# Softmax heads of two attention mixers issued in pairs

## The chip, the cores and the metric

The kernel runs on one NeuronCore of one Trainium2 chip. The time is that of one execution on the device, in microseconds (us). Three runs of the kernel before gave 1333.37, 1333.61 and 1333.80 us, median 1333.61. The execution that was profiled took 1333.43 us, of which the trace covers a span of 1331.7 us.

Five engines work side by side, each through its own instruction queue in order: TensorE (PE; its weight loads are shown as PEld), VectorE (DVE), ScalarE (ACT), GpSimd (POOL) and SyncE (SP), which issues the transfers of the weights.

## The reference, cut to what matters

A decoder trunk of two layers on 256 tokens of width 1024. Each layer is a SwiGLU block, a mixer block with three token mixers side by side, a cross attention and a second SwiGLU block. The change touches two of the three mixers, which end in an ordinary softmax attention with heads of 64 features:

```python
# FoX, 6 heads: causal, with a decay c per head
logits = q @ k.T * 64**-0.5 + c[:, :, None] - c[:, None, :]
o_fox = softmax(where(causal, logits, -inf)) @ v
# DSA, 5 heads: only the 64 keys that an indexer picked for each query
o_dsa = softmax(where(picked & causal, q @ k.T * 64**-0.5, -inf)) @ v
# stick-breaking, 5 heads, is the third mixer and has no softmax
```

All arithmetic is float32. The dense projections are made of three TensorE passes each over a high and a low part of both factors (in the profile a pass is one matmul of line 139, 140 or 141); scores, transposes and value products of the mixers are plain float32.

## The kernel before

`mixer_cross(l)` writes one layer's mixers and cross attention. The 256 queries are two tiles of 128, and causality leaves 128 keys for the first and 256 for the second, so that one head's scores are one tile of 128 x 384 (`Q0`, `Q1`).

Heads go by two. A feature tile of 128 partitions holds two heads, 64 partitions each, and a head's score matmuls therefore read 64 partitions: partitions 0 to 63 for the first head of the two, 64 to 127 for the second. There are two per head, 128 and 256 columns wide (lines 664 and 668 for FoX, where line 664 adds the decay first; line 553 in `scores` for DSA; line 781 for stick-breaking). In this text the score matmuls of one head are a score run. FoX has three pairs of heads, DSA two pairs and a single head, stick-breaking the same.

Then, for each head by itself: DVE adds the mask from PSUM into an SBUF tile (lines 674 and 676, or 698), and `softmax_pv` (line 588) does the rest: maxima (594, DVE), exponentials with their sums (69, ACT), reciprocals (597) and scaling (599, DVE), three transposes of 128 x 128 (602, PE), one copy to SBUF (604, ACT), and `pv`: two value products into the PSUM tile that both heads share (611 and 612, PE). After both heads, `hsplit` splits the result for the output projection (154, DVE and ACT).

PE does not wait for these chains: dense projections that do not depend on them stand between the pieces, and their weights are prepared all the while, the high part by ACT (line 92), the low part by DVE or, for every third one, by POOL (line 86).

What sets the order. The source is traced in program order, and a planner then arranges each engine's queue when the program is built. It takes work in traced order where that is ready by its own estimate, and fills with later work where not. Three things tie its hands here: PSUM has two banks for scores (`qk`), two for transposes (`tr`) and one for value products (`ops`); there are five SBUF tiles `w384` for probabilities; and the helper `issue_after(x)` queues what its block issues on the engine of `x` behind `x`.

Of the kernel before, what the change touches and what calls it, by code (L numbers as in the profile page):

```python
# [9 lines left out]
F32 = mybir.dt.float32  # L10
F32R = mybir.dt.float32r
I32 = mybir.dt.int32
AF = mybir.ActivationFunctionType
OP = mybir.AluOpType
AX = mybir.AxisListType
# [17 lines left out]
def trunk(ctx: ExitStack, tc: tile.TileContext, x, mem, positions, ffn1_norm, ffn1_w_gu, ffn1_w_down,  # L33
# [3 lines left out]
    PE, ACT, DVE, POOL, SP = nc.tensor, nc.scalar, nc.vector, nc.gpsimd, nc.sync  # L37
# [10 lines left out]
    def qk_ps():  # L48
        return psum.tile([128, 512], F32, name="qk", bufs=2)

    def tr_ps():
        return psum.tile([128, 512], F32, name="tr", bufs=2)

    def o_ps():
        return psum.tile([128, 512], F32, name="ops", bufs=1)
# [11 lines left out]
    def tact(*a, **k):  # L67
        with tc.issue_after(tabs["load"].ins):
            i = ACT.activation(*a, **k)  # L69
        tabs["ops"].append(i)  # L70
# [89 lines left out]
    ident = consts.tile([128, 128], F32, name="ident")  # L160
# [55 lines left out]
    def scaled(k, src, h, lo, gi):  # L216

        g = gcol[:, gi * 8 + k:gi * 8 + k + 1]
        i = ACT.activation(h, src, AF.Copy, scale=g)
        DVE.scalar_tensor_tensor(lo, src, g, h.bitcast(F32), op0=OP.mult, op1=OP.subtract)  # L220
        return i
# [29 lines left out]
    with tc.tile_pool(name="start", bufs=1) as st:  # L251
# [10 lines left out]
        for k in (0, 1, 4, 5):  # L262
            ps = (tr_ps, qk_ps)[k // 4]()
            xps[k], xps[k + 2] = ps[:, :256], ps[:, 256:]
        ps = o_ps()
# [5 lines left out]
        for k in range(KD):  # L271
            last = scaled(k, xps[k], xh[k], xl[k], GI["ffn1"])
# [185 lines left out]
    Q0, Q1 = (0, 128), (128, 384)  # L458

    def mixer_cross(l):  # L460
# [4 lines left out]
        with tc.tile_pool(name="mix", bufs=1) as mp:  # L465
# [8 lines left out]
            def w384():  # L474
                return mp.tile([128, 384], F32, name="w384", bufs=5)
# [28 lines left out]
            def proj_feat(cls, bank=acc_ps):  # L504

                w = load_w([W[:, a:b] for a, b in cls])
                ps = bank()
                for s in range(sum(b - a for a, b in cls) // 128):
                    for k in range(KD):
                        mm3(ps[:, s * 256:(s + 1) * 256], cols(w[k], s), xg[k], k == 0, k == KD - 1)  # L510
                return ps
# [51 lines left out]
            for t in range(2):  # L563
                DVE.tensor_scalar(w8[:, t], pss[t][:, 256:264], rc[t], float(np.float32(8 ** -0.5)) * 0.125,
                                  op0=OP.mult, op1=OP.mult)
# [19 lines left out]
            POOL.tensor_tensor(dmask, dmask, cmask, op=OP.add)  # L585


            def softmax_pv(lg, v, h, ot):

                nm = mp.tile([128, 2], F32, name="nm", bufs=4)  # L590
                sm = mp.tile([128, 2], F32, name="sm", bufs=4)
                p = lg
                for t, (c0, c1) in enumerate((Q0, Q1)):
                    DVE.tensor_reduce(nm[:, t:t + 1], lg[:, c0:c1], axis=AX.X, op=OP.max, negate=True)
                    tact(p[:, c0:c1], lg[:, c0:c1], AF.Exp, bias=nm[:, t:t + 1], accum_out=sm[:, t:t + 1])
                rs = mp.tile([128, 2], F32, name="rsm", bufs=4)
                DVE.reciprocal(rs, sm)
                for t, (c0, c1) in enumerate((Q0, Q1)):
                    DVE.tensor_scalar(p[:, c0:c1], p[:, c0:c1], rs[:, t:t + 1], None, op0=OP.mult)
                ps = tr_ps()  # L600
                for j in range(3):
                    PE.transpose(ps[:, j * 128:(j + 1) * 128], p[:, j * 128:(j + 1) * 128], ident)  # L602
                pT = w384()
                ACT.activation(pT, ps[:, :384], AF.Copy)
                pv(ot, v, h, pT[:, 0:256], pT[:, 256:384])

            def pv(ot, v, h, p0, p1):

                o = ot[:, h % 2 * 256:(h % 2 + 1) * 256]
                c = slice(h // 2 * 128, h // 2 * 128 + 128)  # L610
                PE.matmul(o, v[0][:, c], p0, start=True, stop=False)  # L611
                PE.matmul(o[:, 128:256], v[1][:, c], p1, start=False, stop=True)  # L612

            def tok_v(pss, n):
                res = []
                for t in range(2):
                    v = mp.tile([128, 384], F32, name="vtok", bufs=4)
                    ACT.activation(v[:, :n], pss[t][:, :n], AF.Copy, scale=rc[t])
                    if n < 384:
                        POOL.memset(v[:, n:], 0.0)  # L620
                    res.append(v)
                return res
# [3 lines left out]
            for c in range(3):  # L626
                ps = proj_feat([(FOX0 + c * 256, FOX0 + (c + 1) * 256)])
# [6 lines left out]
            fv = tok_v(pss, 384)  # L634
# [12 lines left out]
            ps = tr_ps()  # L647
# [12 lines left out]
            for j in range(NFOX // 2):  # L660
                bank = [qk_ps() for _ in range(2)]
                for i, ps in enumerate(bank):
                    for c in (0, 256):
                        PE.matmul(ps[:, c:c + 256], sel[:, 2 * j + i], cneg, start=c == 0, stop=False)
                for c, n in ((0, 128), (256, 256)):
                    for i, ps in enumerate(bank):
                        b = slice(64 * i, 64 * i + 64)
                        PE.matmul(ps[:, c:c + n], fqk[j][b, c // 2:c // 2 + 128], fqk[3 + j][b, 0:n],  # L668
                                  start=False, stop=c == 256)
                ot = o_ps()  # L670
                for i, ps in enumerate(bank):
                    h = 2 * j + i
                    lg = w384()
                    DVE.scalar_tensor_tensor(lg[:, 0:128], ps[:, 0:128], cq[:, 0, h:h + 1], cmask[:, 0:128],
                                             op0=OP.add, op1=OP.add)
                    DVE.scalar_tensor_tensor(lg[:, 128:384], ps[:, 256:512], cq[:, 1, h:h + 1], cmask[:, 128:384],
                                             op0=OP.add, op1=OP.add)
                    softmax_pv(lg, fv, h, ot)
                ofox.append(hsplit(ot, 2))


# [8 lines left out]
            dv = tok_v(proj_tok(DSA0 + 640, 320), 320)  # L690
            odsa = []
            for j in range(3):
                nh = 2 if j < 2 else 1
                bank = scores(dT[0][j], dT[1][j], nh)
                ot = o_ps()
                for i, ps in enumerate(bank):
                    lg = w384()
                    DVE.tensor_tensor(lg, ps[:, :384], dmask, op=OP.add)
                    softmax_pv(lg, dv, 2 * j + i, ot)
                odsa.append(hsplit(ot, nh))  # L700

            gates = []
# [51 lines left out]
            for i, lst in enumerate((sq, sk)):  # L754
                ps = proj_feat([(SB0 + 320 * i, SB0 + 320 * i + 256)])
                for s in range(2):
                    o = t1()
                    DVE.scalar_tensor_tensor(o, ps[:, s * 256:(s + 1) * 256], (0.125, 1.0)[i], r[:, :256],
                                             op0=OP.mult, op1=OP.mult)
                    lst.append(o)  # L760
            ps = proj_feat([(SB0 + 256, SB0 + 320), (SB0 + 576, SB0 + 640)])
# [7 lines left out]
            for j in range(3):  # L769
# [31 lines left out]
                ot = o_ps()  # L801
# [8 lines left out]
            for k in range(0, KD, 2):  # L810
                mi = mp.tile([128, 2, 256], F32, name="mi", bufs=2)
                SP.dma_start(mi, mem[0, :, k * 128:(k + 2) * 128].rearrange("(t p) n -> p t n", p=128))
                ps = transposed([mi[:, t] for t in range(2)], 0)
# [24 lines left out]
            for c in range(4):  # L838
                w = load_w([w_out[l][:, c * 256:(c + 1) * 256]])
                for s in range(2):  # L840
                    ps = acc_ps()
# [24 lines left out]
            qT, pr, pT, vm, oc = [], [], [], [], []  # L866
# [37 lines left out]
            for c in range(4):  # L904
                w = load_w([ca_w_o[l][:, c * 256:(c + 1) * 256]])
                for s in range(2):
                    ps = acc_ps()
# [40 lines left out]
```

## Time and profile before

| | |
|---|---|
| median of three runs | 1333.61 us |
| the profiled execution | 1333.43 us, span 1331.7 us |
| PE busy | 1312.3 us, 99% of the span |
| weight loads (PEld) | 1276.6 us, 96% |
| DVE, ACT, POOL busy | 68%, 56%, 22% |
| granted TensorE clock | 0.9 or more of full speed in each of the 40 slices |
| chain that ended last | PE 88%, DVE 5%, ACT 2%, DMA 2% |

A row of the timeline is one instruction or a few equal ones that follow each other. A matmul's row lasts from its start to the end of its results, and the next one starts long before that: what a matmul costs PE is the distance from its start to the start of the next. Idle time in brackets counts only what lies behind the modelled end of the row before, so that a wait costs PE somewhat more than the bracket says. The order on PE, DVE, ACT and POOL changes between 259 and 412 us (layer 0) and between 910 and 1062 us (layer 1) and nowhere else; the stretches shown below reach a little further, 262 to 430 and 914 to 1080 us, to the end of the mixers' merge.

### The profile page before, as it was taken

Reading aid. Unit: us, or ns where it says so; the run is one execution under the profiler, and the core shown is the slowest. Engines: PE = TensorE matmul, PEld = TensorE weight load, DVE = VectorE, ACT = ScalarE, POOL = GpSimd, SP = SyncE. Lnnn points to the kernel's source line nnn. Section 1 sums busy time; section 2 is a strip of 40 time slices with the busy share of each in tenths; the row PEclk is TensorE's granted clock in tenths of the full one; section 3 lists DMA queues with packets and bytes.
Section 4 is the critical chain, followed back from the end, with each engine's and each line's share of the span. In section 5 each row is a group of like instructions: output and inputs, shape, how many; then the busy total and the mean of one; then the engine's idle time right before and its main releaser. Section 6 shows DMA issues by size and latency. Waiting matters only on the chain.

```text
span 1331.7 us, 26302 instructions
## 1 busy us (share of the span) xinstructions
PE 1312.3 (99%) x10746; PEld 1276.6 (96%) x10746; DVE 903.5 (68%) x1389; ACT 746.3 (56%) x1191; POOL 299.0 (22%) x267
## 2 busy tenths in 40 slices
PE   8999999999999999999999999999999999999997
PEld 7999998999899999999999999999989999999987
DVE  7866656975778876665666666569667787766644
ACT  6555544454766575554565554544557756655543
POOL 3211114421323222111121110334223230311100
PEclk9999999999999999999999999999999999999999
DMA  7665754544545555666655565646454565466551
GB/s 254 191 193 190 223 150 150 177 140 151 163 135 194 159 187 162 194 200 201 198 190 190 190 206 179 203 124 194 127 153 136 159 205 178 164 196 198 195 184 64
DMA packets 220712, 234.65 MB, mean 176 GB/s; under 512 B 8656, under 2 KB 209968, under 8 KB 220592
## 3 DMA queue, kind: packets, MB, share of 16 engines
q1 hardware_dynamic: 219904, 231.87, 54.7%
q8 instruction: 84, 1.38, 0.4%
q10 hardware_dynamic: 448, 0.57, 0.1%
q0 software_dynamic: 240, 0.55, 0.1%
q14 instruction: 36, 0.29, 0.1%
HBM read 231.91 MB, written 1.05 MB: 175 GB/s over the span
## 4 chain that ended last, share of the span: by engine, by line
PE 88%; DVE 5%; DMA 2%; ACT 2%; issue 2%; POOL 1%; SPq 0%; DVEq 0%; ACTq 0%; POOLq 0%
PE acc L139 27%; PE acc L140 27%; PE acc L141 27%; DVE wl L86 2%; PE qk L553 1%; PE ops L611 1%; ACT wh L92 1%; DMA wraw<-in_ffn_w_gu_dram 1%; DVE t L154 1%; PE qk L668 1%; DVE sc L583 0%; PE ops L612 0%; PE tr L602 0%; DMA wraw<-in_w_sb_out_dram 0%; POOL it L527 0%
## 5 line engine op out<-in xcount | busy, mean ns | idle before, releaser
L86 DVE TENSOR_TENSOR wl<-wraw,wh 128x1024 fp32r<-128x1024 f32 (+4 forms) x427 | 507.5, 1192 | 229.1 <-ACT wh L92 219.2
L92 ACT ACTIVATE wh<-wraw 128x1024 fp32r<-128x1024 f32 (+4 forms) x471 | 465.4, 994 | 262.2 <-PE acc L140 163.9
L141 PE MATMUL acc<-xh,wl 128*128 128x256 f32 x2032 | 563.8, 278 | 1.1 <-DVE wl L86 1.1
L140 PE MATMUL acc<-xl,wh 128*128 128x256 f32 x2032 | 564.0, 278 | 0.0
L139 PE MATMUL acc<-xh,wh 128*128 128x256 f32 x2032 | 563.0, 278 | 0.0
L141 PEld LDWEIGHTS acc<-xh,wl 128*128 128x128 f32 x2032 | 381.8, 188 | 3.3 <-DVE wl L86 1.5
L139 PEld LDWEIGHTS acc<-xh,wh 128*128 128x128 f32 x2032 | 381.3, 188 | 2.7 <-issue 2.7
L140 PEld LDWEIGHTS acc<-xl,wh 128*128 128x128 f32 x2032 | 382.2, 188 | 1.4 <-issue 1.0
L383 POOL TENSOR_TENSOR hm<-sg,gu 128x256 f32<-128x256 f32 x88 | 85.0, 967 | 385.3 <-ACT sg L69 385.3
L141 PE MATMUL acc<-hh,wl 128*128 128x256 f32 x528 | 145.3, 276 | 0.0
L140 PE MATMUL acc<-hl,wh 128*128 128x256 f32 x528 | 145.3, 276 | 0.0
L139 PE MATMUL acc<-hh,wh 128*128 128x256 f32 x528 | 144.3, 276 | 0.0
L86 POOL TENSOR_TENSOR wl<-wraw,wh 128x1024 fp32r<-128x1024 f32 (+4 forms) x44 | 90.6, 2059 | 228.9 <-ACT wh L92 208.5
L69 ACT ACTIVATE sg<-gu 128x256 f32<-128x256 f32 x88 | 36.7, 417 | 120.1 <-DVE gu L379 120.1
L141 PEld LDWEIGHTS acc<-hh,wl 128*128 128x128 f32 x528 | 99.1, 188 | 0.0
L140 PEld LDWEIGHTS acc<-hl,wh 128*128 128x128 f32 x528 | 99.1, 188 | 0.0
L139 PEld LDWEIGHTS acc<-hh,wh 128*128 128x128 f32 x528 | 98.4, 188 | 0.0
L379 DVE TENSOR_TENSOR gu<-acc,rs_r 128x512 f32<-128x512 f32 x88 | 60.3, 686 | 42.6 <-PE acc L141 42.4
L230 POOL TENSOR_TENSOR sqa<-sqa,sq 128x256 f32<-128x256 f32 x54 | 51.1, 945 | 148.7 <-ACT sq L225 147.3
L153 ACT ACTIVATE hh<-hm 128x256 fp32r<-128x256 f32 x88 | 36.1, 410 | 54.1 <-POOL hm L383 54.1
L154 DVE TENSOR_TENSOR hl<-hm,hh 128x256 fp32r<-128x256 f32 x88 | 37.0, 421 | 42.6 <-ACT hh L153 42.4
L141 PE MATMUL acc<-wh,xl 128*128 128x320 f32 (+1 forms) x192 | 61.4, 320 | 0.0
(283 smaller groups left out, 2002.6 us busy)
## 6 DMA issues: line engine op xcount, KB each, us to landing
wraw<-in_ffn_w_gu_dram SPq DMA_DIRECT2D x87, 1024.0 KB, 5.3
wraw<-in_w_in_dram SPq DMA_DIRECT2D x34, 1024.0 KB, 5.3
wraw<-in_ffn_w_down_dram SPq DMA_DIRECT2D x28, 896.0 KB, 4.8
wraw<-in_ffn_w_down_dram SPq DMA_DIRECT2D x18, 1024.0 KB, 5.2
wraw<-in_w_in_dram SPq DMA_DIRECT2D x20, 640.0 KB, 4.1
wraw<-in_ca_w_kv_dram SPq DMA_DIRECT2D x8, 1024.0 KB, 5.0
wraw<-in_w_out_dram SPq DMA_DIRECT2D x8, 1024.0 KB, 5.0
wraw<-in_ca_w_q_dram SPq DMA_DIRECT2D x4, 1024.0 KB, 5.2
```

Source lines behind the costliest of these rows:

```text
L69: i = ACT.activation(*a, **k)
L86: share["last"] = eng.tensor_tensor(lo, raw, h.bitcast(F32), op=OP.subtract)
L92: ACT.activation(h, raw, AF.Copy)
L139: PE.matmul(ps, a[0], b[0], start=first, stop=False)
L140: PE.matmul(ps, a[0], b[1], start=False, stop=False)
L141: PE.matmul(ps, a[1], b[0], start=False, stop=last)
L153: ACT.activation(h, src, AF.Copy)
L154: DVE.tensor_tensor(lo, src, h.bitcast(F32), op=OP.subtract)
L230: POOL.tensor_tensor(n, sqacc[0], sq, op=OP.add)
L379: DVE.tensor_tensor(gu, ps.rearrange("p (i n) -> p i n", i=2), rb2(r), op=OP.mult)
L383: POOL.tensor_tensor(hm, sg, gu[:, 1], op=OP.mult)
L553: PE.matmul(ps[:, c:c + n], q[b, qs], k[b, 0:n], start=True, stop=True)
```

## The change

`softmax_pv` takes the score tiles of both heads of a pair (or the one of the last DSA head) and runs in three passes: normalise all heads, then transpose all heads and copy each, then all value products. The two mixers collect their tiles in `lgs` and call it once for each pair. Two `issue_after` blocks are put around the transposes and the value products; they name an instruction of DVE and one of ACT, while the blocks hold PE instructions alone.

```diff
-            def softmax_pv(lg, v, h, ot):
+            def softmax_pv(lgs, v, h0, ot):
...
+                for p in lgs:
+                    nm = mp.tile([128, 2], F32, name="nm", bufs=4)
+                    sm = mp.tile([128, 2], F32, name="sm", bufs=4)
+                    for t, (c0, c1) in enumerate((Q0, Q1)):
+                        DVE.tensor_reduce(nm[:, t:t + 1], p[:, c0:c1], axis=AX.X, op=OP.max, negate=True)
+                        tact(p[:, c0:c1], p[:, c0:c1], AF.Exp, bias=nm[:, t:t + 1], accum_out=sm[:, t:t + 1])
+                    rs = mp.tile([128, 2], F32, name="rsm", bufs=4)
+                    DVE.reciprocal(rs, sm)
+                    for t, (c0, c1) in enumerate((Q0, Q1)):
+                        last = DVE.tensor_scalar(p[:, c0:c1], p[:, c0:c1], rs[:, t:t + 1], None, op0=OP.mult)
+                pTs = []
+                for p in lgs:
+                    ps = tr_ps()
+                    with tc.issue_after(last.ins):
+                        for j in range(3):
+                            PE.transpose(ps[:, j * 128:(j + 1) * 128], p[:, j * 128:(j + 1) * 128], ident)
+                    pT = w384()
+                    last_copy = ACT.activation(pT, ps[:, :384], AF.Copy)
+                    pTs.append(pT)
+                with tc.issue_after(last_copy.ins):
+                    for i, pT in enumerate(pTs):
+                        pv(ot, v, h0 + i, pT[:, 0:256], pT[:, 256:384])
...
+                lgs = []
                 for i, ps in enumerate(bank):
...
-                    softmax_pv(lg, fv, h, ot)
+                    lgs.append(lg)
+                softmax_pv(lgs, fv, 2 * j, ot)
```

No instruction is added or taken away. What moves is the order, and three places show it. Names carry buffer numbers: `qk_3606` and `qk_3607` are the score banks of the two heads of one pair.

PE, layer 0, the second DSA pair. Before, the first head's score run stands alone among the projections (`acc`), and the second head's comes after 50 more rows:

```order
L141 MATMUL acc_4073<-xh3_85,wl_4066 128x256
L139 MATMUL acc_4073<-xh4_86,wh_4069 128x256
L553 MATMUL qk_3606<-t1_3470,t1_3376 128x128
L553 MATMUL qk_3606<-t1_3470,t1_3376 128x256
L140 MATMUL acc_4073<-xl4_94,wh_4069 128x256
L141 MATMUL acc_4073<-xh4_86,wl_4070 128x256
```

Now:

```order
L140 MATMUL acc_3882<-xl3_93,wh_3874 128x256
L141 MATMUL acc_3882<-xh3_85,wl_3875 128x256
L553 MATMUL qk_3606<-t1_3470,t1_3376 128x128
L553 MATMUL qk_3606<-t1_3470,t1_3376 128x256
L553 MATMUL qk_3607<-t1_3470,t1_3376 128x128
L553 MATMUL qk_3607<-t1_3470,t1_3376 128x256
L139 MATMUL acc_3882<-xh4_86,wh_3878 128x256
```

Both heads' scores now follow each other, and an earlier projection (`acc_3882` in place of `acc_4073`) lies around them.

PE, layer 1, the first stick-breaking pair (`qk_12365`, `qk_12366`), which comes after DSA. Before, a DSA head's value products cut the first head's run in two, and the second head's run stands elsewhere:

```order
L139 MATMUL acc_12505<-osp_11404,wh_12481 128x256
L781 MATMUL qk_12365<-t1_12182,t1_12245 128x256
L611 MATMUL ops_11735<-w384_11752,vtok_11670 128x256
L612 MATMUL ops_11735<-w384_11752,vtok_11673 128x128
L781 MATMUL qk_12365<-t1_12182,t1_12245 128x128
L140 MATMUL acc_12505<-osp_11405,wh_12481 128x256
```

Now (line 781 has become 792):

```order
L141 MATMUL acc_12306<-wh_12301,xl7_97 128x320
L792 MATMUL qk_12365<-t1_12182,t1_12245 128x256
L792 MATMUL qk_12366<-t1_12182,t1_12245 128x256
L792 MATMUL qk_12365<-t1_12182,t1_12245 128x128
L792 MATMUL qk_12366<-t1_12182,t1_12245 128x128
L139 MATMUL acc_12485<-osp_11286,wh_12477 128x256
```

The value products are gone from between, since DSA is over by then, and the two heads stand together.

PE, layer 0, the transposes of the last, single DSA head (`w384_3663`; `osp` is the split output of a mixer, `mi` the memory tokens). Before:

```order
L611 MATMUL ops_3612<-w384_3649,vtok_3547 128x256
L612 MATMUL ops_3612<-w384_3649,vtok_3550 128x128
L602 MATMUL tr_3675<-ident_73,w384_3663 128x128
L243 MATMUL tr_4454<-ident_73,mi_4452 128x128 x4
L602 MATMUL tr_3675<-ident_73,w384_3663 128x128 x2
L139 MATMUL acc_4432<-osp_3163,wh_4404 128x256
```

Now (line 602 has become 606):

```order
L141 MATMUL acc_4010<-xh5_87,wl_4007 128x256
L606 MATMUL tr_3675<-ident_73,w384_3663 128x128
L139 MATMUL acc_4010<-xh6_88,wh_4006 128x256
L606 MATMUL tr_3675<-ident_73,w384_3663 128x128 x2
L140 MATMUL acc_4010<-xl6_96,wh_4006 128x256
L141 MATMUL acc_4010<-xh6_88,wl_4007 128x256
```

They have moved from the merge of the FoX output (`acc_4432`) to an earlier projection (`acc_4010`), with projection matmuls before, between and behind them.

## Rows read from the trace of the kernel before

**Rows 1.** The page, busy time by engine.
```profile
PE 1312.3 (99%) x10746; PEld 1276.6 (96%) x10746; DVE 903.5 (68%) x1389; ACT 746.3 (56%) x1191; POOL 299.0 (22%) x267
```

**Rows 2.** Busy us by stretch; last three columns: granted clock, DMA share, GB/s.
```profile
262.00:430.00 168.00, 165.22 (x1330) 158.47 (x1330) 123.09 (x194) 105.64 (x190) 47.52 (x31) 1.00 0.51 156
914.00:1080.00 166.00, 163.81 (x1316) 156.94 (x1315) 124.56 (x202) 107.45 (x189) 53.75 (x32) 1.00 0.51 156
469.00:479.00 10.00, 10.00 (x61) 8.90 (x60) 5.66 (x13) 7.75 (x17) 0.00 (x0) 1.00 0.65 213
```

**Rows 3.** Timeline of PE, waits: start, duration, row, [idle before <-releaser].
```profile
343.13 0.33 PE L602 MATMUL tr<-ident,w 128*128 128x128 f32 x1 [0.39 <-DVE w L599]
344.50 0.39 PE L139 MATMUL acc<-osp,wh 128*128 128x256 f32 x1 [0.38 <-DVE t L726]
...
425.69 0.39 PE L140 MATMUL acc<-t,wh 128*128 128x256 f32 x1 [0.66 <-DVE t L154]
...
996.47 0.33 PE L602 MATMUL tr<-ident,w 128*128 128x128 f32 x1 [0.20 <-DVE w L599]
996.64 0.60 PE L243 MATMUL tr<-ident,mi 128*128 128x128 f32 x4
997.07 0.38 PE L602 MATMUL tr<-ident,w 128*128 128x128 f32 x2
998.22 0.39 PE L139 MATMUL acc<-osp,wh 128*128 128x256 f32 x1 [0.77 <-DVE t L726]
...
1078.06 0.38 PE L140 MATMUL acc<-t,wh 128*128 128x256 f32 x1 [1.05 <-DVE t L154]
```

**Rows 4.** Timeline of PE: both heads' score runs together; then two heads' value products.
```profile
365.11 0.28 PE L139 MATMUL acc<-xh,wh 128*128 128x256 f32 x1
365.32 0.93 PE L781 MATMUL qk<-t,t 64*128 64x256 f32 x8
...
366.40 0.28 PE L141 MATMUL acc<-xh,wl 128*128 128x256 f32 x1
...
366.65 0.28 PE L140 MATMUL acc<-xl,wh 128*128 128x256 f32 x1
366.77 0.59 PE L611 MATMUL ops<-az,vtok 128*128 128x256 f32 x2
...
368.19 0.28 PE L139 MATMUL acc<-xh,wh 128*128 128x256 f32 x1
```

**Rows 5.** Timeline of PE, layer 0: one head's score run between projections.
```profile
312.78 0.28 PE L141 MATMUL acc<-xh,wl 128*128 128x256 f32 x1
...
313.23 0.28 PE L139 MATMUL acc<-xh,wh 128*128 128x256 f32 x1
313.44 0.92 PE L553 MATMUL qk<-t,t 64*128 64x128 f32 x4
...
314.51 0.28 PE L141 MATMUL acc<-xh,wl 128*128 128x256 f32 x1
```

**Rows 6.** Timeline of PE, layer 1: a score run cut by value products.
```profile
989.52 0.28 PE L139 MATMUL acc<-osp,wh 128*128 128x256 f32 x1
...
991.84 0.28 PE L141 MATMUL acc<-osp,wl 128*128 128x256 f32 x1
```

**Rows 7.** Timeline of DVE, layer 0: one DSA head, mask add and scaling.
```profile
310.95 0.56 DVE L698 TENSOR_TENSOR w<-qk,dmask 128x384 f32<-128x384 f32 x1
...
313.95 0.55 DVE L599 TENSOR_SCALAR w<-w,rsm 128x128 f32<-128x128 f32 x2
```

**Rows 8.** Timelines of POOL and DVE, layer 0: a low part beside a scaling.
```profile
284.62 2.38 POOL L86 TENSOR_TENSOR wl<-wraw,wh 128x1024 fp32r<-128x1024 f32 x1 [7.69 <-DVE rsm L597]
284.64 2.71 DVE L599 TENSOR_SCALAR w<-w,rsm 128x128 f32<-128x128 f32 x2
```

**Rows 9.** Timeline of PE, layer 0, cross attention: a run of transposes.
```profile
469.62 1.03 PE L890 MATMUL tr<-ident,t 128*128 128x128 f32 x8
470.49 1.04 PE L890 MATMUL qk<-ident,t 128*128 128x128 f32 x8
```

More of the change, by code (lines that the diff above doesn't have):

```diff
@@ L585, in mixer_cross @@
             POOL.tensor_tensor(dmask, dmask, cmask, op=OP.add)
-            def softmax_pv(lg, v, h, ot):
[L590 to L605, printed above, removed]
+            def softmax_pv(lgs, v, h0, ot):
[21 more added lines that the diff above has]
+                        pv(ot, v, h0 + i, pT[:, 0:256], pT[:, 256:384])
@@ L695, in mixer_cross @@
                 ot = o_ps()
+                lgs = []
                 for i, ps in enumerate(bank):
@@ L698, in mixer_cross @@
                     DVE.tensor_tensor(lg, ps[:, :384], dmask, op=OP.add)
-                    softmax_pv(lg, dv, 2 * j + i, ot)
+                    lgs.append(lg)
+                softmax_pv(lgs, dv, 2 * j, ot)
                 odsa.append(hsplit(ot, nh))
```

## The prediction

> **What bounds the kernel now.** The page's list of engines comes first: PE is busy for 1312.3 us, 99% of the span [rows 1], and no other engine comes near. So PE's own queue sets the time, and an edit can act in two ways only: on how long PE's instructions take, and on the gaps in which PE waits. [...] Then PE's timeline, which shows where these gaps are. There are nine. Four belong to one place in each layer, the transposes of the last DSA head and the matmul behind them (0.39, 0.38, 0.20 and 0.77 us, sum 1.74); two to the end of the merge, where PE waits for the last split (0.66 and 1.05) [rows 3]; the other three share what is left, 4.97 - 1.74 - 1.71 = 1.52 us. A gap costs more than its bracket: the second of the two transposes at 997.07 starts 0.11 later, and from there to 998.22 are 1.04 us where 0.11 is usual, so that a bracket of 0.77 cost 0.93. I add 0.16 to each.
>
> No more than about 5 + 9 x 0.16 = 6.4 us is therefore to be had from waits. The rest must come from PE's work, and the number of instructions is unchanged. So the question is whether any of them costs less in its new neighbourhood.
>
> **What moves and what it costs.** *Transposes and value products.* Four transposes in a run take from 996.64 to 997.07, 0.11 us each [rows 3]. In the group that is there now, one, then four, then two, none costs more for being in a group of one or two. Two heads' value products take 368.19 - 366.65 less two matmuls, 1.54 - 0.23 = 1.31 us [rows 4]; by half, 0.66 each. To issue six transposes or four products together, which is what the change says, I put at nothing: PE does the same work in the same time.
>
> *Score runs.* These change price. PE's step is (313.23 - 312.78) / 4 = 0.1125 us. One head's score run alone takes PE from 313.23 to 314.51, less two steps: 1.28 - 0.225 = 1.055 us [rows 5]. Both heads' runs next to each other take 366.40 - 365.11, less two steps: 1.29 - 0.225 = 1.065 us [rows 4]. The second head is free when it follows at once: the two read different halves of the partitions, and PE works on both. It is free in the order first head, first head, second head, second head too, since that is how the four stand there. Pairing the softmax makes the planner ask for both score banks at once, and the order shows four pairs joined that were apart: the second DSA pair and the first stick-breaking pair, in both layers. Each saves 2 x 1.055 - 1.065 = 1.045 us, together 4.18.
>
> In layer 1 the stick-breaking run was cut in two besides: from 989.52 to 991.84, less two steps and a head's products, 2.32 - 0.225 - 0.66 = 1.44 us [rows 6], 0.38 over a whole run. That goes as well. In the third FoX pair of layer 0 the new order issues the first head's narrow matmul, then two decay matmuls, then the other three: the pair is joined, but cut. It saves between nothing and 1.045 us; I take 1.045 - 0.38 = 0.66, the price of the cut just seen. The other pairs stay as they were. Sum of PE's work: 4.18 + 0.38 + 0.66 = 5.2 us less.
>
> *Waits that go.* At the four places of the last DSA head nothing stood between its value products and its transposes that PE could do meanwhile. In the new order projection matmuls lie before, between and behind these transposes, and the merge that waited with them comes later than DSA. I count all four as gone: 1.74 + 4 x 0.16 = 2.4 us. If the cover failed, they would come back, no more. The waits at the end of the merge are a chain behind the last eviction, whose order is untouched; they stay.
>
> *Waits that come.* The change adds none by name, but PE must find both heads normalised where it found one. Queued behind a transpose that waits is all of PE. One head's chain on DVE, from mask add to the end of the scaling, takes 314.50 - 310.95 = 3.55 us with exponentials on ACT in between [rows 7]. Two heads in the same queues take at least one more scaling, 4.1 us, and at most twice the time, 7.1. Against this stands the PE work that the new order puts between the last score and the first transposes. It is shortest for the first DSA pair of layer 0: 34 steps and a joined score run, 34 x 0.1125 + 1.065 = 4.9 us. There the wait is between 0 and 2.2 us, and I take 1. For the first DSA pair of layer 1 it is 6.4 us by the same count, and for the other ten groups 9 to 15, above the upper bound.
>
> What can still hold a chain up is a neighbour on DVE. At 284.64 the two scalings of a head took 2.71 us in place of the 0.55 of [rows 7], while POOL's subtraction ran from 284.62 to 287.00 [rows 8]: 2.16 us more. They ended at 287.35, so that at least one of them could finish only when POOL was done. [...]
>
> POOL is busy for 47.52 of 168 us and 53.75 of 166 [rows 2], some 30%. Of the twelve groups of both layers 3 to 4 would be hit, at half the price of 2.16 us on average, 4 us in all, but the groups have 2 us and more in hand. I take 1 us for it, and 0 to 8 for both kinds of wait together.
>
> **The sum.** 1333.43 (the profiled execution, 0.18 below the median of the runs) - 5.2 - 2.4 + 2.0 = 1327.8 us, 0.4% less.
>
> **The rivals.**
>
> *All of it, without new waits.* For it: the long distances above. 1333.4 - 5.2 - 2.4 = 1325.8, and with the cut FoX run fully joined and the three small waits gone, 1333.4 - 5.6 - 2.4 - 2.0 = 1323.4.
>
> *Given back at the merge.* PE reaches the merges earlier by 2.5 us and more in each layer, and both waits there are released by DVE [rows 3]. If DVE's queue sets that moment, and not the chain, the score gain returns as wait: 1333.4 - 2.4 + 1 = 1332.0, no change. For it: DVE is the busiest engine behind PE, 123.09 of 168 us [rows 2]. Against it: that is 73%, and the softmax and stick-breaking work of DVE moves forward with its chains.
>
> *The joined runs do not pay.* The second head's matmuls can wait in the run for their bank or operands, and the price of [rows 4] is from stick-breaking alone. Then 1333.4 - 2.4 + 2.0 = 1333.0, no change. Against it: the order of both kernels has such runs of line 553 too.
>
> *Slower: both heads behind one lock.* With the scalings of two heads side by side, one blocked scaling delays six transposes. The place is the scaling of each of the twelve groups, the price 2.16 us. The gain of 5.2 + 2.4 - 1 = 6.6 us is eaten by three hits in full, and it decides for slower by 0.2% from 9.3 us on, between four and five hits. Six would give 1333.4 - 6.6 + 13.0 = 1339.8. For it: [rows 8] show such a hit just ahead of a head's transposes. Against it: the hits must fall where there is no lead.
>
> [...]
>
> **How the numbers follow.** Forecast 1325 to 1331: 0.58. Better than that: 0.10. Given back: 0.12. Joined runs that do not pay: 0.06. Slower by the lock: 0.13. By the clock: 0.01. A difference under 0.2%, 2.7 us, can't be told from none here. So faster 0.68, same 0.18, slower 0.14. The range reaches from 1323.5, the best case, to 1335, past the two cases without gain and up to the first hits of the lock that outweigh it; it leaves out 0.04 below and 0.14 above. Of the forecast alone it would be 1325 to 1331.
>
> **What would show it.** Right: the four joined score runs at 1.06 us each; no wait at the last DSA head's transposes; PE's idle time in the two stretches at or below 5 us; all transposes and products at their old price. Wrong: gaps of 1 us and more before transposes with DVE's scaling as releaser and POOL's subtraction beside it (the lock); longer gaps at the end of the merge (given back); second heads in joined runs that cost 0.3 us or more (the price); a clock below 1.00.

## The result and the profile after

The changed kernel takes 1322.96 us (median of four runs, 1322.72 to 1323.02). The ratio to the kernel before is 0.992, with a 95% interval of 0.9908 to 0.9931: 10.7 us less than 1333.70, the median of four runs. The forecast was 1327.8 us with a range from 1323.5, so the direction was right, the size was half of what came, and the time lies just below the range. The profiled execution took 1323.02 us, 10.41 less than that of before. All times here are medians; one execution of e10_late_4, which took 5323.44 us, is left out.

The same views as before, of the kernel after. First the page's list of engines, then the table by stretch over the same work (it begins and ends some us earlier now):

```profile
PE 1305.2 (99%) x10746; PEld 1273.2 (96%) x10746; DVE 894.0 (68%) x1389; ACT 746.3 (56%) x1191; POOL 295.8 (22%) x267
```

```profile
262.00:424.30 162.30, 161.71 (x1331) 156.72 (x1330) 116.04 (x191) 106.64 (x191) 48.38 (x31) 1.00 0.53 162
908.40:1069.60 161.20, 160.37 (x1315) 155.23 (x1314) 121.60 (x202) 106.01 (x187) 51.13 (x33) 1.00 0.52 162
```

The two stretches are 5.7 and 4.8 us shorter than in [rows 2], and nothing outside them changed by more than 0.1. PE's idle time in them fell from 4.97 us (2.78 in layer 0 and 2.19 in layer 1, span less PE busy in [rows 2]) to 0.59 + 0.83 = 1.42 us. DVE is busy for 9.5 us less over the span with the same instructions. Three waits are left, from PE's timeline:

```profile
420.05 0.38 PE L140 MATMUL acc<-t,wh 128*128 128x256 f32 x1 [0.59 <-DVE t L154]
921.38 0.47 PE L671 MATMUL qk<-cneg,sel 128*128 128x256 f32 x2 [0.27 <-DVE w L684]
1067.65 0.39 PE L140 MATMUL acc<-t,wh 128*128 128x256 f32 x1 [0.56 <-DVE t L154]
```

Two are the ends of the merges, one is new (the decay of a FoX pair, at 921.38, which waits for a score bank that DVE's mask add frees). The four at the last DSA head [rows 3] are gone, as forecast. But the three small ones are gone too, and the end of layer 1's merge waits half as long. A joined score run, the second DSA pair of layer 0, PE's timeline:

```profile
299.08 0.28 PE L141 MATMUL acc<-xh,wl 128*128 128x256 f32 x1
299.29 0.93 PE L553 MATMUL qk<-t,t 64*128 64x128 f32 x8
300.15 0.39 PE L139 MATMUL acc<-xh,wh 128*128 128x256 f32 x1
300.37 0.28 PE L140 MATMUL acc<-xl,wh 128*128 128x256 f32 x1
...
301.63 0.49 PE L606 MATMUL tr<-ident,w 128*128 128x128 f32 x3
...
302.20 0.27 PE L606 MATMUL tr<-ident,w 128*128 128x128 f32 x1
...
302.43 0.38 PE L606 MATMUL tr<-ident,w 128*128 128x128 f32 x2
```

From 299.08 to 300.37, less two steps, are 1.29 - 0.225 = 1.065 us for both heads, the price of [rows 4]. Below it are the six transposes of the pair before: three, then one, then two, with projections between. "Issued together" in the source is not together on PE.

The two table loads that bracket the sigmoids show a larger move, which the prediction had not looked at. They are ACT's line 64, behind the last exponential of DSA and of stick-breaking. Timeline of ACT, layer 0, before:

```profile
341.80 1.28 ACT L64 ACT_TABLE_LOAD   x1
...
398.90 1.28 ACT L64 ACT_TABLE_LOAD   x1
```

and after:

```profile
314.36 1.28 ACT L64 ACT_TABLE_LOAD   x1
...
383.83 1.28 ACT L64 ACT_TABLE_LOAD   x1
```

DSA ends 27.4 us earlier and stick-breaking 15.1, while PE's projections moved by 5.7 at most. Before, PE waited right behind these points: at 344.50 [rows 3] and in this row, both released by DVE's gate product (line 726), which reads the sigmoids.

```profile
403.23 0.36 PE L139 MATMUL acc<-osp,wh 128*128 128x256 f32 x1 [0.51 <-DVE t L726]
```

### The profile page after: what moved, and what is told of

Same layout as the page of the kernel before. It is cut to its first block, busy times and chain, and to the rows that moved or that the text cites. A ratio compares the mean times of both kernels' runs of the same rounds, so it can differ in the third digit from the quotient of the medians.

```text
span 1321.3 us, 26329 instructions
## 1 busy us (share of the span) xinstructions
PE 1305.2 (99%) x10746; PEld 1273.2 (96%) x10746; DVE 894.0 (68%) x1389; ACT 746.3 (56%) x1191; POOL 295.8 (22%) x267
## 4 chain that ended last, share of the span: by engine, by line
PE 94%; DVE 2%; DMA 1%; issue 1%; POOL 1%; ACT 1%; DVEq 0%; ACTq 0%; POOLq 0%
PE acc L139 29%; PE acc L141 28%; PE acc L140 28%; DVE wl L86 1%; PE qk L553 1%; PE ops L618 1%; PE qk L675 1%; DMA wraw<-in_ffn_w_gu_dram 1%; DVE t L154 1%; PE ops L619 1%; PE tr L606 0%; POOL it L527 0%; DMA wraw<-in_w_in_dram 0%; PE qk L861 0%; PE qk L792 0%
## 5 line engine op out<-in xcount | busy, mean ns | idle before, releaser
L86 DVE TENSOR_TENSOR wl<-wraw,wh 128x1024 fp32r<-128x1024 f32 (+4 forms) x427 | 512.7, 1204 | 224.2 <-ACT wh L92 210.9
```

The costliest lines, as they stand in the source:

```text
L86: share["last"] = eng.tensor_tensor(lo, raw, h.bitcast(F32), op=OP.subtract)
```

## The experiments

Two theories of the waits. Theory A, a lead: when heads go one by one, the mixers' chains end too late for the projections that stand behind them; in the new order they end earlier. Rival B, meetings: the waits came from operations of DVE that met a subtraction on POOL, as in [rows 8], and the new order happens to have fewer. B had support at once. This view of one tile's instructions gives count and min/median/max in ns of the scaling, before and after:

```profile
L599 DVE TENSOR_SCALAR w<-w,rsm x44: 281/344/2447, 262.2 to 996.3; 128x128 f32<-128x128 f32 x22, 128x256 f32<-128x256 f32 x22
```

```profile
L600 DVE TENSOR_SCALAR w<-w,rsm x44: 261/314/350, 264.9 to 965.5; 128x128 f32<-128x128 f32 x22, 128x256 f32<-128x256 f32 x22
```

Before, 8 of the 44 took over 0.5 us; after, none did. That holds for the scalings alone: the DVE operations of stick-breaking meet POOL in both kernels.

**What of the edit makes the order.** One edit on the kernel before, in both mixers:

```diff
                 for i, ps in enumerate(bank):
                     lg = w384()
                     DVE.tensor_tensor(lg, ps[:, :384], dmask, op=OP.add)
-                    softmax_pv(lg, dv, 2 * j + i, ot)
+                    lgs.append(lg)
+                for i, lg in enumerate(lgs):
+                    softmax_pv(lg, dv, 2 * j + i, ot)
```

> The kernel before with one edit: the mask adds of both heads of a pair are written ahead of the first head's softmax; maxima, exponentials, transposes, copy and value products stay head by head. Theory A (the gain comes from the order in which the planner sets PE's queue once the second head's mask add no longer stands behind the first head's copy, and not from grouped transposes or grouped value products): the order on all five engines is that of the changed kernel, so 1323.0 us, within 0.5. Rival B (grouping six transposes and four products is worth something in itself): between 1326 and 1333.7 us.

Measured: 1323.60 us, ratio 0.9921 (0.9906 to 0.9936), the whole of the gain. Instruction for instruction the order on the five engines is that of the changed kernel; only buffer numbers differ. The planner gives the same order when the second head's mask add is written behind the first head's transposes, and the old one when it is written behind the first head's copy. Without the two `issue_after` blocks the order of the changed kernel stays as it is. (None of these three versions was timed.) So neither grouped transposes nor grouped value products nor the blocks gave anything: the second head's mask add (one DVE instruction in DSA, two in FoX), written ahead of one copy, did it all.

**What a joined run saves.** In the changed kernel, three times:

```diff
-                        b = slice(64 * i, 64 * i + 64)
+                        b = slice(0, 64)
```

> The changed kernel with one number changed: the second head of every pair reads its scores from partitions 0 to 63, those of the first head (so the second head's scores are not its own). Order and instruction counts are unchanged. Theory A (two adjacent heads cost 1.06 us because PE works on both halves of the partitions at once): the 16 fully joined pairs of both layers rise from 1.06 us towards 2.11, each by 0.7 to 1.05 us, 11 to 17 us in all: 1334 to 1340 us. Rival B (a lone head costs 1.055 us because of a fixed price at the two ends of a score run, paid once per run): the joined runs stay near 1.06 us and the time stays at 1323 us.

Measured: 1334.32 us, ratio 1.000 (0.999 to 1.001), 10.7 us above e1_mask_first, which ran beside it. The run of the rows above now, PE's timeline:

```profile
302.73 0.28 PE L141 MATMUL acc<-xh,wl 128*128 128x256 f32 x1
302.94 1.57 PE L553 MATMUL qk<-t,t 64*128 64x128 f32 x8
304.44 0.39 PE L139 MATMUL acc<-xh,wh 128*128 128x256 f32 x1
304.67 0.28 PE L140 MATMUL acc<-xl,wh 128*128 128x256 f32 x1
```

1.94 - 0.225 = 1.71 us. So both were partly right: of the 1.045 us that a joined pair saves, 0.65 come from the two halves of the partitions and 0.40 from a run that begins and ends once instead of twice. 16 pairs x 0.65 and 0.43 for the cut one make 10.8, as measured (10.7); PE's waits are the same in both, 1.4 us.

**Pairs in one mixer alone.** FoX keeps the pairs, DSA hands over single heads, and the other way round:

```diff
-                    lgs.append(lg)
-                softmax_pv(lgs, dv, 2 * j, ot)
+                    softmax_pv([lg], dv, 2 * j + i, ot)
```

> The changed kernel with the pairs in FoX alone; DSA hands its heads to the softmax one by one, mask add and all, as before. Score runs against the kernel before: the first stick-breaking pair joined in both layers (2 x 1.045), its cut in layer 1 gone (0.38), the third FoX pair of layer 0 joined but cut (0.43), a new cut in the second DSA pair of layer 0 (-0.38): 2.5 us less. Theory A (waits go because the mixers' chains end earlier against PE's projections): with half of the pairs the last stick-breaking head still comes earlier, most of the waits at the merges and at the last DSA head go, 3 to 4.5 us: 1326.5 to 1328.5 us. Rival B (waits go because scalings no longer meet POOL's subtractions on DVE): the waits stay wherever a DSA scaling still takes over 0.4 us; 1330 us or more.

> The changed kernel with the pairs in DSA alone; FoX hands its heads to the softmax one by one as before. Score runs against the kernel before: the second DSA pair joined in both layers, the first stick-breaking pair joined in layer 0 (3 x 1.045) and joined but cut in layer 1 (about 0.7), a new cut of the lone DSA head and of a FoX run in layer 0 and (-0.4 to -0.8): 3.1 us less. Theory A (earlier chains): the waits at the last DSA head and two of those at the merges go, 3 to 4 us: 1326.5 to 1328 us. Rival B (fewer meetings of scaling and POOL): FoX scalings still meet POOL as before, 5 of the 8 long scalings stay, and the waits with them: 1330 us.

Measured: 1326.65 us (0.9943, 0.9928 to 0.9958) and 1325.13 us (0.9932, 0.9917 to 0.9947): 7.5 and 9.0 us less, the first as A gave, the second 1.4 us below it, which was not traced. The two don't add up (16.5 against 10.6), since either alone takes away nearly all waits: 1.4 us of brackets are left in both stretches together, as with both. With DSA alone 7 scalings still meet POOL. Timeline of e4_dsa_pairs, layer 1, POOL, then DVE, then PE:

```profile
971.71 2.49 POOL L86 TENSOR_TENSOR wl<-wraw,wh 128x1024 fp32r<-128x1024 f32 x1 [9.73 <-ACT wh L92]
```

```profile
972.69 1.85 DVE L600 TENSOR_SCALAR w<-w,rsm 128x128 f32<-128x128 f32 x2
```

```profile
976.17 0.27 PE L606 MATMUL tr<-ident,w 128*128 128x128 f32 x1
976.43 0.38 PE L606 MATMUL tr<-ident,w 128*128 128x128 f32 x2
```

The scaling lost 1.3 us, and the transposes that need it have no bracket: a meeting without a wait. The changed kernel has one too, in the first stick-breaking pair of layer 1, where this DVE operation took 2.53 us in place of 0.95 beside POOL and the matmuls behind it have no bracket:

```profile
989.74 2.53 DVE L154 TENSOR_TENSOR spl<-az,sph 128x768 fp32r<-128x768 f32 x1
```

Both speak for A.

**Other draws.** The count that gives POOL every third low part, moved by one and by two places, in both kernels:

```diff
         share["pool"] = 3
+        share["n"] += 1
```

> The kernel before with another draw of the low parts: POOL takes every third as before, but counted from one place later, so that other subtractions meet the scalings on DVE. No other edit. Theory A (in the kernel before the mixers' chains end too late for PE, wherever POOL's subtractions fall): the waits at the last DSA head's transposes, behind the sigmoids and at the merges are there again, 4 to 7 us over both layers, and the time is 1332 to 1336 us. Rival B (the waits came from the few scalings and stick-breaking operations that met POOL): the waits move or go with the hits, and the time may fall to 1329 us.

> The same with the count moved by two places. Theory A: 1332 to 1336 us, waits at the same places. Rival B: as low as 1329 us, and other places than in the run moved by one.

> The changed kernel with the count of the low parts moved by one place. Score runs: the third FoX pair of layer 0 falls apart (+0.43), that of layer 1 is joined but cut (-0.43). Theory A (the paired order gives the chains a lead, whatever POOL meets): no waits over 0.5 us except at the end of the two merges, 1321.5 to 1325 us, 8.5 to 12 below the kernel before moved by one. Rival B (this order happened to miss POOL): scalings meet POOL again and 2 to 5 us of waits come back, 1325 to 1328 us.

> The changed kernel with the count moved by two places. Score runs: the third FoX pair joined in full in both layers (-0.6 and -1.03), the second DSA pair apart by three rows in both (+2.09). Theory A: no waits over 0.5 us except at the end of the merges, 1322 to 1325.5 us, 8 to 12 below the kernel before moved by two. Rival B: 1325.5 to 1329 us, with waits behind scalings that took over 0.5 us.

| draw | before, us | after, us | difference | waits before / after, us | scalings over 0.5 us |
|---|---|---|---|---|---|
| as it was | 1333.70 | 1322.96 | -10.7 | 5.0 / 1.4 | 8 / 0 |
| by one | 1335.24 | 1323.73 | -11.5 | 5.9 / 1.5 | 8 / 0 |
| by two | 1346.74 | 1329.89 | -16.9 | 8.8 / 2.8 | 10 / 0 |

(Waits are the brackets of both stretches. A draw also moves work outside them, so only differences within a row count. By two, both kernels missed the time that A gave; the difference is larger than A gave, and part of it is the clock: the kernel before has a mean granted clock of 0.991 to 0.996 in this draw, all others of the table 0.998 or 0.999.) The sign and the places hold in every draw: all three kernels of before wait for the last DSA head's scaling and behind the sigmoids, in both layers. The meetings differ as well, so this does not part A from B.

By two, the changed kernel also missed A's "no waits over 0.5 us": it waits for the second stick-breaking pair in both layers, 0.85 us each. e8_after_n2, layer 0, POOL, DVE and PE:

```profile
362.04 2.41 POOL L86 TENSOR_TENSOR wl<-wraw,wh 128x1024 fp32r<-128x1024 f32 x1
362.73 2.54 DVE L154 TENSOR_TENSOR spl<-az,sph 128x768 fp32r<-128x768 f32 x1 [0.36 <-ACT sph L153]
365.32 0.50 PE L805 MATMUL qk<-spl,negu 128*128 128x512 f32 x1 [0.85 <-DVE spl L154]
```

That is a wait as B has it, in the changed order: the operation lost 1.6 us, and here its reader had no such lead.

**No meetings at all.** In the kernel before:

```diff
-        share["pool"] = 3
+        share["pool"] = 0
```

> The kernel before with all low parts of the mixers on DVE: POOL has none, so that no scaling can meet one. DVE gets some 16 more subtractions of 1.2 us in each layer. Theory A (the chains of single heads end too late for PE by themselves): the waits of PE for the last DSA head's scaling and behind the sigmoids are still there, 1.5 us or more in each layer, though no scaling takes over 0.4 us: 1334 to 1345 us. Rival B (the waits were made by scalings that met POOL): these waits are gone, and what remains is for low parts (line 86): 1327 to 1334 us.

Measured: 1342.85 us, ratio 1.0069 (1.0054 to 1.0084). The time lies where A put it, but says little, since the granted clock fell to 0.50 in both layers of the profiled execution (340 to 346 and 1000 to 1010 us); in the kernel before it is 1.00 in both stretches [rows 2]. The scaling, and PE's waits in layer 0 (us in total, times, longest):

```profile
L599 DVE TENSOR_SCALAR w<-w,rsm x44: 268/314/351, 265.1 to 1007.0; 128x128 f32<-128x128 f32 x22, 128x256 f32<-128x256 f32 x22
```

```profile
PE tr L602 <- DVE w L599: 1.2, 1, 1.2
PE acc L140 <- DVE t L154: 0.7, 1, 0.7
PE ops L611 <- DVE w L698: 0.6, 1, 0.6
PE acc L139 <- DVE t L726: 0.5, 1, 0.5
```

No scaling takes over 0.351 us, and the waits for the scaling and behind the sigmoids are there, the first larger than in the kernel before (1.2 for 0.39); together 8.0 us of brackets. So PE waits there without any meeting. But DVE's list is longer here by the subtractions it took over, so that this run alone doesn't show what made the waits of the kernel before.

**Where the waits of the kernel before come from.** Its own trace goes further. First the last DSA head of layer 1, ACT and then DVE, ahead of PE's wait at 996.47 [rows 3]:

```profile
994.14 0.49 ACT L604 ACTIVATE w<-tr 128x384 f32<-128x384 f32 x1 [0.99 <-PE tr L602]
995.46 0.56 DVE L783 TENSOR_TENSOR zm<-qk,smask 128x384 f32<-128x384 f32 x1 [1.91 <-PE qk L781]
996.13 0.55 DVE L599 TENSOR_SCALAR w<-w,rsm 128x128 f32<-128x128 f32 x2
```

ACT copied the transposes of the head before, and only then, at 994.53, began the last head's exponentials; DVE stood idle for 1.91 us ahead of this head's scaling, which took its usual 0.55. PE, which released the copy and the mask add of 995.46, had no wait of its own between 925 and 996 us, so that no meeting has a part in this. In layer 0 DVE met POOL in a scaling at 335.59, but stood idle for 1.07 us behind it, before the last head's maxima at 340.48, so that this loss did not reach PE's wait at 343.13 either; and the sigmoids of 344.50 and 998.22 stand behind the same exponentials. Ahead of the wait at 403.23 POOL had done nothing for 16 us, and DVE had been waiting for PE at 395.91, so that no earlier loss was carried over:

```profile
403.16 1.30 POOL L728 TENSOR_TENSOR t<-t,t 128x512 f32<-128x512 f32 x1 [16.19 <-DVE t L726]
```

These five waits, 2.2 of the 5.0 us of brackets, are late chains, as A has it. The wait at 359.72, for the first stick-breaking pair of layer 0, is not. POOL, DVE, ACT and PE:

```profile
355.38 2.60 POOL L86 TENSOR_TENSOR wl<-wraw,wh 128x1024 fp32r<-128x1024 f32 x1 [3.44 <-ACT wh L92]
355.64 3.15 DVE L787 SCALAR_TENSOR_TENSOR az<-zm,az 128x768 f32<-128x768 f32 x1
358.82 0.84 ACT L153 ACTIVATE sph<-az 128x768 fp32r<-128x768 f32 x1 [3.05 <-DVE az L787]
359.72 0.50 PE L793 MATMUL qk<-sph,negu 128*128 128x512 f32 x1 [0.83 <-ACT sph L153]
```

The DVE operation lost 2.2 us (its like takes 0.95), ACT stood idle for 3.05 us until it was done, and PE lost 1.00 us: without the meeting the operand would have been there in time. Without meetings (e9_before_nopool) this wait is not in the list, and in the other draws the waits for a stick-breaking pair stand behind such a meeting too. So A holds for the waits at the last DSA head and behind the sigmoids, B for this one; what made the two waits at the ends of the merges and the small one for a low part was not traced.

**How long the lead is.** The changed kernel with transfers in the lone stick-breaking head, two and four rounds of:

```diff
+                    SP.dma_start(zf[:, 1], zf[:, 0])
+                    SP.dma_start(zf[:, 0], zf[:, 1])
                 tact(az, zm, AF.Exp)
```

> The changed kernel with a delay in the lone stick-breaking head of each layer: ahead of its last exponential its tile is copied four times to and fro by SP's transfers, which load no computing engine. [...] The sigmoids that the merge waits for stand behind this exponential on ACT: the table switch ahead of them is at 383.83 us in the changed kernel, and the merge wants them some 9 us later. Theory A (a lead of about 9 us): a delay below 9 us costs nothing, 1323 to 1324 us; what is over 9 us comes back as waits of PE at the merge. Rival B (a late chain does no harm, PE has other work): 1323 us.

> [...] Theory A: 3 to 11 us of waits at the merge in each layer, on the matmuls that read the split outputs and released by DVE's gate product: 1329 to 1345 us, and the wait is the delay less about 9 us. Rival B: 1323 to 1325 us.

Measured: 1329.35 us (0.9965, 0.9952 to 0.9979) and 1351.82 us (1.0133, 1.0118 to 1.0148). The 3 to 11 us of waits that A gave with eight copies rest on the author's estimate of one transfer, which no run had shown. In layer 0 a transfer took 3.3 us with four and 3.2 us with eight (median from issue to landing; 2.1 to 4.9 in both). The exponential on ACT and PE's waits behind it, layer 0, with four and with eight:

```profile
397.33 0.52 ACT L69 ACTIVATE az<-zm 128x384 f32<-128x384 f32 x1 [3.32 <-DMA zm<-zm]
```

```profile
397.90 0.70 PE L618 MATMUL ops<-az,vtok 128*128 128x256 f32 x2 [1.21 <-ACT az L69]
400.66 0.37 PE L139 MATMUL acc<-osp,wh 128*128 128x256 f32 x1 [1.24 <-DVE t L737]
```

```profile
410.01 0.52 ACT L69 ACTIVATE az<-zm 128x384 f32<-128x384 f32 x1 [14.17 <-DMA zm<-zm]
```

```profile
410.58 1.22 PE L618 MATMUL ops<-az,vtok 128*128 128x256 f32 x2 [13.26 <-ACT az L69]
```

Undelayed, this exponential starts at 383.29. 14.0 us later costs 1.2 us at the value products and brings back the wait behind the sigmoids (1.24); another 12.7 us cost another 12.1. Up to some 13 us of delay are free, and then, in layer 0, it is one for one: A, though the lead is longer than the 9 us expected. In layer 1 eight copies cost only 6.2 us at the value products, where the planner had put more merge work ahead of them. It knows of the transfers and had moved the value products back in both layers, so this is the lead that it could make use of, not that of an untouched order. A part of the times is the clock: with eight it was 0.50 from 411 to 416 us, behind the wait; with four its mean from 262 to 430 us was 0.99.

**All pairs joined.** Order edges on PE in the changed kernel; in `scores`, and alike in the other places:

```diff
-                    for i, ps in enumerate(bank):
+                    for i in reversed(range(nh)):
...
+                            if lead:
+                                es.enter_context(tc.issue_after(lead.ins))
+                            m = PE.matmul(bank[i][:, c:c + n], q[b, qs], k[b, 0:n], start=True, stop=True)
+                        lead = lead or m
```

> The changed kernel with every score pair joined by order edges on PE: in the indexer, DSA and stick-breaking the first head's matmuls are queued behind the second head's first one, in FoX both heads' score matmuls behind the second head's decay matmuls. Against the changed kernel that joins two indexer pairs of layer 0 (2 x 1.045), the second FoX pair of both layers and the third of layer 1 (3 x 1.03) and takes the cut out of the third of layer 0 (0.6): 5.8 us less, 1317.2 us, if no wait comes. Rival (a first head that must wait for the second bank holds up PE): each such wait costs up to the distance between the two heads' mask adds, 0.7 us, and the time stays at 1320 us or more.

Measured: 1319.13 us, ratio 0.9887 (0.9872 to 0.9901): faster than both kernels, 4 us below the changed one by the ratios. The second FoX pair of layer 0, and what came back, PE's timeline:

```profile
260.39 0.93 PE L681 MATMUL qk<-t,t 64*128 64x128 f32 x8
...
266.72 0.89 PE L611 MATMUL tr<-ident,w 128*128 128x128 f32 x5 [0.96 <-DVE w L605]
```

The runs are joined as expected (the sum of their prices is 5.8 us lower). The wait at 266.72 is not the rival's, which spoke of banks: four scalings from 263.21 took 3.91 us while POOL worked until 266.43. Here is the prediction's lock: five scalings over 0.5 us in this order, two of them here, and PE waits behind these two and none of the others.

## Why the prediction was wrong

Its steps against the trace, start to start, in us of the profiled executions:

| step | forecast | measured |
|---|---|---|
| transposes and value products together | 0 | 0 |
| score runs joined, cuts | -5.2 | -5.0 |
| waits at the last DSA head | -2.4 | -2.4 |
| waits that come | +2.0 | +0.4 |
| waits that stay: three small, two at the merges' ends | 0 | -2.6 |
| rest, in small steps | | -0.8 |
| sum | -5.6 | -10.4 |

The score runs were right in price and number; of their sum only the cut FoX pair was off (0.43 for 0.66). Their reason was half right (e2_same_half). The edit as its title names it was rightly put at nothing, but the prediction gave the pairing of the softmax as what makes the planner ask for both banks at once, and that was too wide: the mask adds alone do it.

The step that failed is the one on waits: of the 4.8 us between forecast and measurement (10.4 - 5.6), 2.6 are waits that were to stay and 1.6 are waits that were to come. The 0.8 us of the last row were not traced. The step took the waits one by one, by the instruction that each stood behind. The transposes of the last DSA head lost theirs, as their neighbours in the order said. The rest were kept, "a chain behind the last eviction, whose order is untouched; they stay", and the small ones were not looked into. But the chains behind them end at other times now. (The starts below are those of the waiting matmul in the kernel before; the costs count from the start of the matmul ahead.) The wait at 403.23 (0.67) is for gates behind the last stick-breaking exponential, 15.1 us earlier against 5.7 on PE: no longer late, and e10_late_4 brings it back. The wait at 359.72 (1.00) was made by a meeting with POOL and went because its DVE operation meets none in the new order. That is luck of the draw: by two, the changed kernel has two such waits for another pair. The wait at 921.83 (0.34, for a low part) went, and the merge's end in layer 1 fell from 1.22 to 0.72; neither was traced to a cause.

The new waits were bounded from two heads' chains at 4.1 to 7.1 us against 4.9 us of PE work. The first DSA pair of layer 0 took, from mask add to the end of the scaling, 3.95 us (296.66 to 300.61), hardly more than one head's 3.55 [rows 7], since ACT's exponentials of one head run beside DVE's maxima of the other. The one wait that came (0.27, 0.44 start to start) is for a score bank. The lock stood as a cost to come, 1 us, for the scalings alone: the author's estimate, with half of 2.16 us as the mean price of a hit. No run shows that half, and no scaling of the changed kernel took over 0.350 us. It was there as a credit, too, in stick-breaking, whose wait of 1.00 us it had made; to the eight long scalings of the kernel before [rows 8] no wait was traced. In e4_dsa_pairs, as at 284.64 in [rows 8], the scalings that met POOL's subtraction ended only behind it (at 974.54, POOL's at 974.20). But the 1.3 us lost there cost PE nothing, since their reader had a lead.

The case that came was a rival, "all of it, without new waits", with its lower end of 1323.4 us; a time below the forecast was given 0.10. That this end comes so near is in part luck: it had the three small waits gone, without a reason, but also the cut FoX run joined in full (0.4 us), which stayed cut, and it had neither the merge of layer 1 nor the small steps. The slower cases did not come, neither the lock nor the clock, which had a chance of 0.01: the granted clock is 1.00 in both stretches, as it was before in the 10 us [rows 2] around the 16 transposes of [rows 9].

## What to carry over

Where one engine is full and others feed it in long chains, ask of a new order not only which wait loses its neighbour but how much earlier each chain ends against the full engine's work: a chain that ends 15 us earlier takes its later waits along. And ask of each wait, before it is kept or struck, whether its chain was late by itself or by a meeting on a shared resource: the first kind goes with the order, the second with the next draw. The score runs of two heads were worth putting next to each other: apart they cost 2 x 1.055 = 2.11 us, together 1.065 us on different halves of the partitions and 1.71 us on the same half (e2_same_half), so that one begin and end less was worth 0.40 us by itself. When an edit does several things, look in the order for the smallest one that makes the same order; here it was the place of the second head's mask add, and the grouping that gave the change its name did nothing.

## What the runs showed of the hardware

A score run of one head (two matmuls of 64 rows, 384 columns) cost 1.055 us [rows 5], of two heads on both halves 1.065 [rows 4], of two heads on one half 1.71 (e2_same_half).

In e6_before_n2 the granted clock fell to 0.50 behind a short wait: PE waited for 1.68 us at the last DSA head of layer 1 and a little later for 1.15. Its timeline, then the table by stretch (granted clock third from the right):

```profile
1004.21 0.33 PE L603 MATMUL tr<-ident,w 128*128 128x128 f32 x1 [1.68 <-DVE w L600]
...
1006.62 0.58 PE L139 MATMUL acc<-osp,wh 128*128 128x256 f32 x1 [1.15 <-DVE t L727]
1007.00 0.42 PE L140 MATMUL acc<-osp,wh 128*128 128x256 f32 x1
```

```profile
1005.00:1006.50 1.50, 0.47 (x3) 0.07 (x1) 1.04 (x3) 1.50 (x4) 0.00 (x0) 0.50 0.16 38
1006.50:1009.00 2.50, 2.38 (x11) 2.38 (x12) 1.26 (x3) 2.47 (x4) 0.00 (x0) 0.50 0.25 85
```

The granted clock was 0.50 before the second wait was over, and from 1007.00 to 1010.84 a step took 0.21 us in place of 0.11: 18 slow steps, some 1.8 us on top of the waits. But in layer 0 of the same execution two waits at the same place, the second even longer, left it at 1.00:

```profile
345.02 0.33 PE L603 MATMUL tr<-ident,w 128*128 128x128 f32 x1 [1.68 <-DVE w L600]
347.44 0.38 PE L139 MATMUL acc<-osp,wh 128*128 128x256 f32 x1 [1.43 <-DVE t L727]
```

```profile
347.00:350.00 3.00, 2.56 (x22) 2.56 (x23) 1.58 (x3) 2.97 (x5) 0.00 (x0) 1.00 0.24 81
```

So the length of these waits alone did not decide it, and what did is not shown here. In the kernel before, with 0.20 and 0.77 us at the place in layer 1 [rows 3], the clock of the stretch was 1.00 [rows 2].
